# Second products of a four-layer trunk: unit order in layers 2 and 3, order of sum loads, DRAM sums of layer 1, low parts at the seams

## The chip, the cores and the metric

One core of one Trainium2 chip runs the whole program. The metric is the device time of one execution in microseconds (us), from its start to its end. The profiler's span, from the first to the last instruction, is a little shorter than that time. The core has TensorE (PE: matmuls, with weight loads shown apart as PEld), VectorE (DVE), ScalarE (ACT), GpSimd (POOL) and SyncE (SP). SP does nothing here but issue DMAs; ACT and POOL issue a few. A letter q behind an engine's name (SPq, DVEq) means its instruction queue.

## The reference

Four layers act on x of 256 rows and 1024 columns in float32. A layer adds a mixer's output to x (retention, convolution, stick-breaking, retention again) and then that of a feed-forward product:

```python
def squared_relu_mlp(xn, w1, w2):
    h = jax.nn.relu(xn @ w1)
    return (h * h) @ w2
...
        x = x + m
        x = x + squared_relu_mlp(rms_norm(x, norm_ffn[i]), ffn_w1[i], ffn_w2[i])
    return rms_norm(x, final_norm)
```

w1 is 1024 x 4096, w2 4096 x 1024. The change touches the second product, (h * h) @ w2, of each layer, and the places where its end meets the next layer (the seams).

## The kernel before

**Weights.** Every weight is read from DRAM in tiles called raw, 128 x 2048 float32 (1 MB), in an order fixed ahead of time (the plan); a chunk is one such tile, and chunks are numbered through the program. A float32 product is made of three passes: a weight or an activation is cut into a rounded high part and what is left, the low part, and high x high, high x low and low x high are summed (`triple` in `down`). For a weight tile ACT writes the high part (a CAST into wh) and DVE the low part (a subtraction into wl). Pools hold three raw tiles, five wh, five wl and ten 128 x 512 tiles named t. A tile is loaded again once its last reader is done, so a late reader on DVE or ACT delays an SP load, and all loads behind it on SP's queue.

**Second product.** `down` (L770 on) adds up four accumulators C[t, c] (t: half of the rows, c: half of the columns). w2 has 16 blocks kb of 256 rows, and the table MIXED gives the order in which most are used. A *plain* block takes two weight tiles, made by `unit`, and 24 matmuls of 128 x 512. A *fast* block is done as one step of Strassen's scheme (`fast_unit`, L425 on): seven products P1 to P7 of three matmuls each, on seven 128 x 512 operands. Of these, two lie in the first half of the raw tile (low part: L399), two in its second half (L436), and three are sums of blocks of w2, named t3, t2 and t4 (L435 makes the high part, L436 the low part). P5 takes t3, P6 t2, P7 t4; t4 is always t2 plus a block of raw and is made on DVE (L463). P1, P4, P5 and P6 go to four accumulators of their own (mis). Behind the last entry of MIXED, kb 15, ACT copies P1 and P4 out of them (e1 and e5, L827 and L828), and DVE combines all into C (L829 to L834). The remaining plain blocks, REST, follow for c = 0 and then for c = 1.

**Sums made ahead in DRAM.** For a fast block, up to three of its sums of weights are made in DRAM by `make_sums` (L402 on): ACT issues a DMA that writes one block into a DRAM buffer, m or two times over, and POOL issues a DMA that adds other blocks onto it. AHEAD lists, for each layer, at which chunk each of these jobs is issued, and m: 1 gives only the second-half operand t1, 2 also t3, 3 also t2. `unit_hi` then loads raw in two parts, 768 KB from w2 and 256 KB from the buffer, and t3 and t2 as 256 KB loads (t<-sums). With m of 1 or 0, `sum_ahead` (L415 on) makes t3 in SBUF: SP loads one block into a t tile (L421), and POOL adds the second by DMA (L422); each `fast_unit` starts the next one's.

**Order.** Each engine works through its instructions in order. A scheduler arranges them from the program; `issue_after(x)` puts an instruction behind x.

**Seams.** `middle` (L855 on) passes hooks to `down`, which scale finished accumulators (L875 on ACT, L877 on DVE, L906 on DVE), transpose them on PE (`turn`, L888) and add them to x (`onto`, L895), while the plain blocks of REST still run. The next layer's first weight tiles are made at the same time.

Of the kernel before, what the change touches and what calls it, by code (L numbers as in the profile page):

```python
# [56 lines left out]


FAST = 2 * [(3, 5, 7, 9, 12, 13, 14, 15)] + 2 * [(3, 5, 7, 9, 11, 12, 13, 14, 15)]
MIXED = 2 * [(0, 1, 3, 5, 2, 7, 9, 4, 12, 13, 6, 14, 15)] + 2 * [(0, 1, 3, 5, 2, 7, 9, 11, 4, 12, 13, 14, 15)]  # L60
REST = 2 * [(8, 10, 11)] + 2 * [(6, 8, 10)]
AHEAD = {
    0: [(n, 2) for n in (26, 27, 28, 38, 40, 42, 45)],
    1: [(n, 1) for n in (81, 83, 85, 87, 89, 91)],
    2: [(n, 3) for n in (112, 114, 116, 118, 120, 128, 131, 134, 137)],
    3: [(n, 3) for n in (167, 170, 173, 176, 179, 182, 192, 196, 199)],
}
# [186 lines left out]
class Trunk:  # L254
    def __init__(self, ctx, tc, xT, w, prm, cst, fin, gn, out):
        self.tc, self.nc = tc, tc.nc
        self.w_d, self.out_d, self.x_d, self.fin_d, self.gn_d = w, out, xT, fin, gn
        pool = lambda name, bufs, **k: ctx.enter_context(tc.tile_pool(name=name, bufs=bufs, **k))
        self.cp = pool("cp", 1)
        self.raw = pool("raw", 3)  # L260
        self.wp = pool("wp", 5)
        self.zp = pool("zp", 1)
        self.big = pool("big", 36)
        self.t2 = pool("t2", 10)
        self.colp = pool("colp", 3)
        self.bc = pool("bc", 2)
        self.prp = pool("prp", 3)
        self.dram = pool("dram", 2, space=bass.MemoryType.DRAM)
        self.acc_p = pool("acc", 4, space=bass.MemoryType.PSUM)
        self.mis_p = pool("mis", 4, space=bass.MemoryType.PSUM)  # L270
        self.n = 0
        self.un = 0
        self.rest = self.end = None
        self.sums, self.later, self.made = [], [], {}
        nc = self.nc
        head = self.cp.tile([P, NP0 + 512], F32, name="head", tag="head")
        self.prm0 = head[:, :NP0]
        self.x = [head[:, NP0:]]
        self.prm = self.cp.tile([P, NPCOL - NP0], F32, name="prm", tag="prm")
        self.cst = self.cp.tile([P, CCOL["D"]], F32, name="cst", tag="cst")  # L280
        self.first = [self.raw.tile([P, RAWW], F32, name=f"raw{n}", tag="raw") for n in range(3)]
        self.ones = self.tmp().bitcast(mybir.dt.bfloat16)[:, :512]
        nc.gpsimd.memset(self.ones, 1.0)
        self.warm(11)

        def weights(n, a, b, queue=nc.sync):
            queue.dma_start(self.first[n][:, a:b], w[n][:, a:b])

        weights(0, 0, 512, nc.scalar)
        nc.sync.dma_start(head[:, : NP0 + S], xT[:, : NP0 + S])  # L290
        nc.sync.dma_start(self.x[0][:, S:], xT[:, NP0 + S : NP0 + 512])
        weights(0, 512, 1024)
        for p in range(1, 4):
            self.x.append(self.cp.tile([P, 512], F32, name=f"x{p}", tag=f"x{p}"))
            nc.sync.dma_start(self.x[p], xT[:, NP0 + p * 512 : NP0 + (p + 1) * 512])
            weights(p // 2, p % 2 * 1024, (p % 2 + 1) * 1024)
        for o in range(UPC):
            weights(2, o * 1024, (o + 1) * 1024)
        n = CCOL["D"]
        nc.sync.dma_start(self.cst[:, :n], cst[:, :n])  # L300
        nc.sync.dma_start(self.prm, prm[:, NP0:])
        self.cst_d = cst
        self.cr = {k: self.cp.tile([P, P], F32R, name=f"{k}r", tag=f"{k}r") for k in ("U", "m1", "id", "neg")}
        self.id = self.c("id", P)
# [42 lines left out]
    def unit_hi(self, key):  # L347
        nc = self.nc
        assert PLAN[self.un] == key, (PLAN[self.un], key)
        o = self.un % UPC  # L350
        if o == 0:
            n = self.un // UPC
            if n < len(self.first):
                self.rawt = self.first[n]
            else:
                self.rawt = self.raw.tile([P, RAWW], F32, name=self.nm("raw"), tag="raw")
                h = 1024 if n < 4 else UPC * 1024
                made = self.made.get((key[1], key[3])) if key[2] == "f" else None
                if made:
                    h = 1536  # L360
                parts = [
                    (self.rawt[:, a : a + h], self.w_d[n][:, a : a + h]) for a in range(0, UPC * 1024 // h * h, h)
                ]
                if made:
                    d, m = made
                    parts.append((self.rawt[:, h : h + 512], d[:, :512]))
                    self.fetched = [self.tmp() for _ in range(m - 1)]
                    parts += [(t, d[:, 512 * (a + 1) : 512 * (a + 2)]) for a, t in enumerate(self.fetched)]
                for o, d in parts:
                    load = nc.sync.dma_start(o, d)  # L370
                    if made and key[3] not in FAST[key[1]][:2]:
                        self.tc.keep_in_program_order(load)
            for _ in range(min(2, len(self.later))):
                self.later.pop(0)()
            if self.un // UPC in JOBS:
                self.make_sums(*JOBS[self.un // UPC])
            if self.un // UPC in DECAY:
                i = DECAY.index(self.un // UPC) % RH
                if i == 0:
                    self.decay = self.cp.tile([P, RH * 384], F32, name=self.nm("decay"), tag="decay")  # L380
                n = i * 384
                self.tc.keep_in_program_order(
                    nc.sync.dma_start(self.decay[:, n : n + 384], self.cst_d[:, CCOL["D"] + n : CCOL["D"] + n + 384])
                )
        o = self.un % UPC
        src = self.rawt[:, o * 1024 : (o + 1) * 1024]
        hi = self.wp.tile([P, 1024], F32R, name=self.nm("wh"), tag="wh")
        lo = self.wp.tile([P, 1024], F32R, name=self.nm("wl"), tag="wl")
        n = 512 if self.un < 2 * UPC else 1024
        cuts = [slice(i, i + n) for i in range(0, 1024, n)]  # L390
        for s in cuts:
            nc.scalar.copy(hi[:, s], src[:, s])  # L392
        self.un += 1
        return hi, lo, src, cuts

    def unit_lo(self, u):
        hi, lo, src, cuts = u
        for s in cuts:
            self.lo_ins = self.nc.vector.tensor_sub(lo[:, s], src[:, s], hi[:, s]).ins  # L399
        return hi, lo  # L400


# [23 lines left out]
    def fast_unit(self, name, l, kb):  # L426
# [32 lines left out]
                t2 = self.tmp()  # L459
                nc.vector.tensor_add(t2, t1, b22)  # L460
        t4 = self.tmp()
        parts(t3, t2)
        nc.vector.tensor_add(t4, t2, b21)  # L463
        parts(t4)
        return [out[i] for i in (1, 0, 2, 3, 4, 5, 6)]


# [311 lines left out]
    def down(self, i, h, fast, begin, hook):  # L779
# [15 lines left out]
        C = {}  # L795
# [42 lines left out]
        if i == 0:  # L838
# [7 lines left out]

            self.later = [fetch] * len(self.strips)

        for c in range(2):
            w, late = {}, late_kb[-2] if c else late_kb[-1] + 1  # L850
            steps = [(kb, kk, t) for kb in late_kb if kb < late for kk in range(2) for t in range(2)]
            steps += [(kb, kk, t) for t in range(2) for kb in late_kb if kb >= late for kk in range(2)]
            for kb, kk, t in steps:
                if kb not in w:
                    with self.tc.issue_after(closed) if c else nullcontext():  # L855
                        w[kb] = plain(kb, c)
                if c:
                    hook(C, (kb, kk, t))
                triple(C[t, c], block(2 * kb + kk, t), w[kb][kk], stop=(kb, kk) == (late_kb[-1], 1))
            if c == 0:  # L860
                with self.tc.issue_after(closed):
                    hook(C, 0)
        return C


    def middle(self, i, h, fast, sums, nxt):
# [24 lines left out]
        def onto(p, *t):  # L891
            x, a = (v3(b, 2, S) for b in (self.x[p], pt[p]))
            if t:
                x, a = (b[:, :, t[0] * P : (t[0] + 1) * P] for b in (x, a))
            nc.vector.tensor_add(x, x, a)  # L895

        def hook(C, at):
            if at == "open":
# [4 lines left out]
            if at == 0:  # L903
                for t, op in enumerate((ALU.add, ALU.subtract)):
                    y[t, 0] = self.tmp()
                    nc.vector.scalar_tensor_tensor(  # L906
                        out=y[t, 0], in0=C[t, 0], scalar=r2[:, t : t + 1], in1=y["open", t], op0=ALU.mult, op1=op
                    )
                self.norm_begin()
            if at == (REST[i][1], 0, 0):  # L910
                for t in range(2):
                    turn(t, 0)
                for p in range(2):
                    onto(p)
                    self.norm_pair(p, *nxt, False)
                    self.norm_sq(p, nc.vector)
            if at == (REST[i][-2], 0, 1):
# [4 lines left out]
                    onto(p, 0)  # L922

        C = self.down(i, h, fast, None, hook)
        scaled(C, 1, 1, (slice(0, S), "act"), (slice(S, 512), "dve"))

        def rest():
# [943 lines left out]
```

## Time and profile before

| what | value |
|---|---|
| median of three runs | 1336.99 us (1332.95 to 1337.97) |
| the profiled execution | 1336.21 us |
| its span, first to last instruction | 1334.4 us |
| mean granted TensorE clock | 0.996 |
| busy: PE, DVE, ACT, POOL | 98%, 82%, 66%, 16% |
| DMA queue of SP | 259.74 MB |
| DMA queue of POOL | 31.20 MB |
| DMA queue of ACT | 17.30 MB |

The profile is one execution. Its page has the busy time of each engine, the span cut into slices, and the chain of work that ended last: from the last instruction back, at each step to what released it or to the instruction before it on its engine. Further views of the trace are the waits (who waited for whom, in total, how often, the longest), stretches (busy time of each engine between two times, and the clock granted to TensorE), and the timeline (instructions in order of time, runs of alike ones merged, with the idle time ahead of them and its releaser in brackets). "mis" and "acc" are accumulators, "in_w" the weights in DRAM, "sums" the DRAM buffers, "big" 128 x 512 tiles. A matmul of 128 x 512 is listed with 0.39 us because it overlaps its neighbours; PE starts one every 0.227 us.

### The profile page before, as it was taken

How to read it: one execution, taken by the hardware profiler on the slowest of the kernel's cores; microseconds unless marked ns; L12 is line 12 of the kernel's file. 1: busy time of each engine (PE TensorE's matmuls, PEld its weight loads, DVE VectorE, ACT ScalarE, POOL GpSimd, SP SyncE). 2: the span in 40 equal slices, each digit the busy share in tenths (PEclk: the TensorE clock that was granted, in tenths of full speed). 3: DMA queues.
4: the chain of work that ended last, by engine and by line, in shares of the span. 5: the costliest groups of instructions: out<-in, count | busy, mean ns of one | idle time of the engine just before them, and what ended most of it. 6: DMA issues, size and time to landing. Idle time of an engine off the chain costs nothing.

```text
span 1334.4 us, 20667 instructions
## 1 busy us (share of the span) xinstructions
PE 1311.9 (98%) x7661; PEld 1126.7 (84%) x7661; DVE 1089.1 (82%) x1903; ACT 883.1 (66%) x1451; POOL 213.4 (16%) x240
## 2 busy tenths in 40 slices
PE   9999999999999999989999999999999999999998
PEld 7988888888899898868788898887888888888886
DVE  7988777888888588769888588878898667799977
ACT  7555556886666478856668678866766554667764
POOL 3554421000019010010001110100031101101000
PEclk9999999999999999989999999999999999999999
DMA  8566786887675657788578858997566888569883
GB/s 308 212 209 234 250 254 207 238 259 256 235 296 138 210 173 232 216 218 268 188 218 218 237 171 260 270 287 263 203 222 216 256 252 262 192 215 275 260 290 111
DMA packets 76037, 309.57 MB, mean 232 GB/s; under 512 B 8480, under 2 KB 13728, under 8 KB 52512
## 3 DMA queue, kind: packets, MB, share of 16 engines
q1 hardware_dynamic: 55888, 259.74, 54.9%
q0 software_dynamic: 11520, 31.20, 12.0%
q10 hardware_dynamic: 8528, 17.30, 5.3%
q8 instruction: 60, 0.98, 0.3%
q14 instruction: 41, 0.34, 0.1%
HBM read 301.57 MB, written 45.45 MB: 260 GB/s over the span
## 4 chain that ended last, share of the span: by engine, by line
PE 88%; DMA 6%; DVE 3%; ACT 1%; issue 1%; SPq 1%; DVEq 0%; POOLq 0%; ACTq 0%
PE acc L647 22%; PE acc L643 11%; PE acc L784 11%; PE acc L1220 6%; PE acc L1222 6%; PE acc L1221 6%; PE mis L784 5%; DMA t<-sums 3%; PE acc L627 3%; PE acc L628 3%; PE acc L629 3%; PE mis L647 2%; DVE wl L399 1%; DMA t<-in_w 1%; PE acc L1388 1%; PE mis L643 1%
## 5 line engine op out<-in xcount | busy, mean ns | idle before, releaser
L399 DVE TENSOR_TENSOR wl<-raw,wh 128x1024 fp32r<-128x1024 f32 (+1 forms) x406 | 495.9, 1235 | 97.9 <-ACT wh L392 96.3
L392 ACT CAST wh<-raw 128x1024 fp32r<-128x1024 f32 (+1 forms) x406 | 418.8, 1041 | 193.7 <-PE acc L1222 63.4
L647 PE MATMUL acc<-z,wh 128*128 128x512 f32 x1152 | 399.1, 393 | 0.0
L643 PE MATMUL acc<-z,wl 128*128 128x256 f32 x1152 | 317.7, 280 | 0.0
L647 PEld LDWEIGHTS acc<-z,wh 128*128 128x128 f32 x1152 | 214.2, 187 | 46.8
L643 PEld LDWEIGHTS acc<-z,wl 128*128 128x128 f32 x1152 | 216.9, 189 | 2.4 <-DVE t L672 0.3
L784 PE MATMUL acc<-wh,big 128*128 128x512 f32 x632 | 208.8, 391 | 0.0
L784 PEld LDWEIGHTS acc<-wh,big 128*128 128x128 f32 x632 | 118.8, 188 | 24.5
L1220 PE MATMUL acc<-wh,z 128*128 128x512 f32 x352 | 138.4, 394 | 0.0
L1222 PE MATMUL acc<-wh,z 128*128 128x512 f32 x352 | 137.3, 390 | 0.0
L1221 PE MATMUL acc<-wl,z 128*128 128x512 f32 x352 | 137.2, 390 | 0.0
L784 PE MATMUL acc<-wl,big 128*128 128x512 f32 x316 | 123.3, 390 | 1.6 <-DVE wl L436 1.6
L435 ACT CAST wh<-t 128x512 fp32r<-128x512 f32 x102 | 60.4, 619 | 51.9 <-DMA t<-in_w 12.1
L410 POOL DMA_DIRECT2D sums<-in_w x31 | 27.2, 888 | 373.1 <-DMA sums<-in_w 373.1
L671 ACT COPY t<-acc 128x256 f32<-128x256 f32 x154 | 53.1, 371 | 49.3 <-PE acc L647 47.5
L436 DVE TENSOR_TENSOR wl<-t,wh 128x512 fp32r<-128x512 f32 x102 | 65.9, 687 | 17.0 <-ACT wh L435 16.9
L1220 PEld LDWEIGHTS acc<-wh,z 128*128 128x128 f32 x352 | 66.1, 188 | 15.2 <-issue 2.2
L1222 PEld LDWEIGHTS acc<-wh,z 128*128 128x128 f32 x352 | 66.1, 188 | 14.7 <-issue 0.8
L1221 PEld LDWEIGHTS acc<-wl,z 128*128 128x128 f32 x352 | 66.1, 188 | 13.4
L784 PEld LDWEIGHTS acc<-wl,big 128*128 128x128 f32 x316 | 59.5, 188 | 14.6 <-DVE wl L436 2.4
L784 PE MATMUL mis<-wh,big 128*128 128x512 f32 x168 | 64.1, 396 | 5.9 <-ACT wh L435 5.9
L672 DVE TENSOR_TENSOR t<-acc,t 128x256 f32<-128x256 f32 x154 | 59.5, 419 | 10.4 <-ACT t L671 10.0
(309 smaller groups left out, 2358.8 us busy)
## 6 DMA issues: line engine op xcount, KB each, us to landing
raw<-in_w SPq DMA_DIRECT2D x183, 1024.0 KB, 5.3
raw<-in_w SPq DMA_DIRECT2D x31, 768.0 KB, 5.6
sums<-in_w ACTq DMA_DIRECT2D x25, 512.0 KB, 7.5
sums<-in_w POOLq DMA_DIRECT2D x25, 512.0 KB, 9.1
t<-sums SPq DMA_DIRECT2D x43, 256.0 KB, 6.7
raw<-sums SPq DMA_DIRECT2D x31, 256.0 KB, 5.8
sums<-in_w POOLq DMA_DIRECT2D x24, 256.0 KB, 6.6
strip<-st POOLq DMA_DIRECT2D x36, 128.0 KB, 4.0
```

The lines of the kernel that those rows point to most:

```text
L392: nc.scalar.copy(hi[:, s], src[:, s])
L399: self.lo_ins = self.nc.vector.tensor_sub(lo[:, s], src[:, s], hi[:, s]).ins
L435: nc.scalar.copy(h[:, c], t)
L436: self.lo_ins = nc.vector.tensor_sub(g[:, c], t, h[:, c]).ins
L643: mm = nc.tensor.matmul(ps[m][:, :S], wl[:, kk, cs], a[:, :S], start=first and kk == 0, stop=False, **kw)
L647: nc.tensor.matmul(ps[m], wh[:, kk, cs], a, start=False, stop=last and kk == 3, **kw)
L671: nc.scalar.copy(o[:, s], ps[m][:, S:])
L672: nc.vector.tensor_add(o[:, s], ps[m][:, :S], o[:, s])
L784: mm = nc.tensor.matmul(o, l, r, start=start and n == 0, stop=stop and n == 2, skip_group_check=True)
L1220: nc.tensor.matmul(ps[t], zh[:, s], wh[:, kk], start=k == 0, stop=False, skip_group_check=True)
L1221: nc.tensor.matmul(ps[t], zh[:, s], wl[:, kk], start=False, stop=False, skip_group_check=True)
L1222: nc.tensor.matmul(ps[t], zl[:, s], wh[:, kk], start=False, stop=k == 7, skip_group_check=True)
```

## The change

Five edits.

1. MIXED of layers 2 and 3 is reordered: kb 3 and 5 follow kb 0 directly, and fast blocks stand in groups of at most three.
2. AHEAD of layer 1 had six jobs of m = 1 at chunks 81 to 91; it has seven of m = 2 at chunks 77 to 89. `sum_ahead` is left with one block of layer 1, kb 15.
3. Where t3 and t2 come from DRAM, they are loaded ahead of their raw tile.
4. In `fast_unit` t4 moves back among DVE's instructions: with m = 3 behind the low part of raw's second half, otherwise behind t2's low part. The parts of a block are chained by `issue_after`.
5. At a seam the low parts of the next layer's first tiles are held behind the addition to x of the first two pairs of columns (`hold`), and the last tile of REST for c = 1 is made behind the scaling of C for c = 0 (`first`).

```diff
-MIXED = 2 * [(0, 1, 3, 5, 2, 7, 9, 4, 12, 13, 6, 14, 15)] + 2 * [(0, 1, 3, 5, 2, 7, 9, 11, 4, 12, 13, 14, 15)]
+MIXED = 2 * [(0, 1, 3, 5, 2, 7, 9, 4, 12, 13, 6, 14, 15)] + 2 * [(0, 3, 5, 1, 7, 9, 2, 11, 12, 4, 13, 14, 15)]
...
-    1: [(n, 1) for n in (81, 83, 85, 87, 89, 91)],
+    1: [(n, 2) for n in (77, 79, 81, 83, 85, 87, 89)],
...
-                    parts += [(t, d[:, 512 * (a + 1) : 512 * (a + 2)]) for a, t in enumerate(self.fetched)]
+                    extra = [(t, d[:, 512 * (a + 1) : 512 * (a + 2)]) for a, t in enumerate(self.fetched)]
+                    parts = extra + parts
...
         for s in cuts:
-            self.lo_ins = self.nc.vector.tensor_sub(lo[:, s], src[:, s], hi[:, s]).ins
+            with self.tc.issue_after(self.hold) if self.hold else nullcontext():
+                self.lo_ins = self.nc.vector.tensor_sub(lo[:, s], src[:, s], hi[:, s]).ins
...
         t4 = self.tmp()
-        parts(t3, t2)
-        nc.vector.tensor_add(t4, t2, b21)
-        parts(t4)
+        if m == 3:
+            with self.tc.issue_after(self.lo_ins):
+                self.lo_ins = nc.vector.tensor_add(t4, t2, b21).ins
+        with self.tc.issue_after(self.lo_ins):
+            parts(t3, t2)
+        if m < 3:
+            with self.tc.issue_after(self.lo_ins):
+                nc.vector.tensor_add(t4, t2, b21)
+        with self.tc.issue_after(self.lo_ins):
+            parts(t4)
...
+        first = None
         for c in range(2):
...
                 if kb not in w:
-                    with self.tc.issue_after(closed) if c else nullcontext():
+                    after = first if first and kb == late_kb[-1] else closed if c else None
+                    with self.tc.issue_after(after) if after else nullcontext():
                         w[kb] = plain(kb, c)
...
             if c == 0:
                 with self.tc.issue_after(closed):
-                    hook(C, 0)
+                    first = hook(C, 0)
...
                 for p in range(2):
-                    onto(p)
+                    y["on"] = onto(p)
...
         C = self.down(i, h, fast, None, hook)
+        self.hold = y["on"]
```

The order of three engines shows where instructions stand now. The first place is SP in layer 1, from the load of kb 5's raw tile to that of kb 7's. In the kernel before (the t<-in_w loads at L421 are for POOL's additions):

```order
L370 DMA raw_6749<-in_w 128x1536
L370 DMA raw_6749<-sums_6017 128x512
L370 DMA raw_6798<-in_w 128x2048
L421 DMA t_1330_6618<-in_w 128x512
L421 DMA t_1331_6621<-in_w 128x512
L421 DMA t_1349_6703<-in_w 128x512
L421 DMA t_1365_6756<-in_w 128x512
L370 DMA raw_6832<-in_w 128x1536
L370 DMA raw_6832<-sums_6146 128x512
```

and in the changed one, where line numbers are one or two higher:

```order
L371 DMA raw_6748<-in_w 128x1536
L371 DMA raw_6748<-sums_5763 128x512
L371 DMA raw_6796<-in_w 128x2048
L423 DMA t_1331_6621<-in_w 128x512
L371 DMA t_1347_6697<-sums_5642 128x512
L371 DMA t_1363_6749<-sums_5763 128x512
L371 DMA t_1380_6831<-sums_5893 128x512
L371 DMA raw_6830<-in_w 128x1536
L371 DMA raw_6830<-sums_5893 128x512
```

Three of the four 256 KB loads now read finished sums of DRAM; POOL's DMA behind each of them is gone. The number of loads up to this point is the same.

The second place is DVE in layer 2, two fast blocks that follow each other (kb 7 and 9 in both). Before, t4 of the second (L463) stands ahead of low parts of the first:

```order
L399 TENSOR_TENSOR wl_9910<-raw_9902,wh_9909 128x1024
L463 TENSOR_TENSOR t_2091_9965<-t_2086_9952,raw_9950 128x512
L436 TENSOR_TENSOR wl_9914<-raw_9902,wh_9913 128x1024
L436 TENSOR_TENSOR wl_9919<-t_2073_9903,wh_9918 128x512
L436 TENSOR_TENSOR wl_9919<-t_2074_9904,wh_9918 128x512
L436 TENSOR_TENSOR wl_9926<-t_2079_9917,wh_9925 128x512
L463 TENSOR_TENSOR t_2103_10013<-t_2098_10000,raw_9998 128x512
L399 TENSOR_TENSOR wl_9958<-raw_9950,wh_9957 128x1024
```

Now each block's t4 (L466) stands within the block:

```order
L401 TENSOR_TENSOR wl_9872<-raw_9864,wh_9871 128x1024
L438 TENSOR_TENSOR wl_9876<-raw_9864,wh_9875 128x1024
L466 TENSOR_TENSOR t_2075_9879<-t_2070_9866,raw_9864 128x512
L438 TENSOR_TENSOR wl_9882<-t_2069_9865,wh_9881 128x512
L438 TENSOR_TENSOR wl_9882<-t_2070_9866,wh_9881 128x512
L438 TENSOR_TENSOR wl_9888<-t_2075_9879,wh_9887 128x512
L401 TENSOR_TENSOR wl_9920<-raw_9912,wh_9919 128x1024
```

What DVE waits for at t4 is its own block's t2, which SP loads ahead of that block's raw tile now, and behind it before.

The third place is ACT at the end of layer 0's second product: the last fast block, kb 15 (raw_3864), then the first tiles of REST (raw_3928). Before:

```order
L435 CAST wh_3871<-raw_3864 128x1024
L435 CAST wh_3878<-t_712_3347 128x512
L435 CAST wh_3878<-t_835_3875 128x512
L435 CAST wh_3885<-t_836_3877 128x512
L392 CAST wh_3934<-raw_3928 128x1024
L827 COPY big_3910<-mis_3449 128x512
L392 CAST wh_3950<-raw_3928 128x1024
L828 COPY big_3911<-mis_3450 128x512
```

and now:

```order
L437 CAST wh_3871<-raw_3864 128x1024
L437 CAST wh_3878<-t_712_3347 128x512
L437 CAST wh_3878<-t_835_3875 128x512
L836 COPY big_3910<-mis_3449 128x512
L837 COPY big_3911<-mis_3450 128x512
L437 CAST wh_3885<-t_836_3877 128x512
L393 CAST wh_3934<-raw_3928 128x1024
L393 CAST wh_3950<-raw_3928 128x1024
```

The copies of P1 and P4 (mis_3449 and mis_3450) have moved ahead of the high part of t4 (t_836) and of the first tile of REST. Layer 1 has the same order; in layers 2 and 3 only the copy of P1 stands ahead of t4's high part.

At the seam from layer 1 to layer 2, DVE did the two scalings of L906, three low parts (L399) and then the two additions to x; now the two scalings, one low part and the additions, and three low parts behind them.

More of the change, by code (lines that the diff above doesn't have):

```diff
@@ L272, in __init__ @@
         self.un = 0
-        self.rest = self.end = None
+        self.rest = self.end = self.hold = None
         self.sums, self.later, self.made = [], [], {}
@@ L894, in onto @@
                 x, a = (b[:, :, t[0] * P : (t[0] + 1) * P] for b in (x, a))
-            nc.vector.tensor_add(x, x, a)
+            return nc.vector.tensor_add(x, x, a).ins
         def hook(C, at):
@@ L905, in hook @@
                     y[t, 0] = self.tmp()
-                    nc.vector.scalar_tensor_tensor(
+                    last = nc.vector.scalar_tensor_tensor(
                         out=y[t, 0], in0=C[t, 0], scalar=r2[:, t : t + 1], in1=y["open", t], op0=ALU.mult, op1=op
@@ L909, in hook @@
                 self.norm_begin()
+                return last.ins
             if at == (REST[i][1], 0, 0):
```

## The prediction

> **What bounds the kernel now.** I read the page first: busy time, then the chain that ended last.
>
> ```profile
> PE 1311.9 (98%) x7661; PEld 1126.7 (84%) x7661; DVE 1089.1 (82%) x1903; ACT 883.1 (66%) x1451; POOL 213.4 (16%) x240
> ...
> PE 88%; DMA 6%; DVE 3%; ACT 1%; issue 1%; SPq 1%; DVEq 0%; POOLq 0%; ACTq 0%
> ```
>
> PE is busy for all but 22.5 us of the span of 1334.4, and the change keeps every matmul. So only PE's idle time, and what a slow restart adds to it, can be won. The view of PE's waits says where that is (what PE waited for: us in total, times, longest):
>
> ```profile
> PE mis L784 <- ACT wh L435: 5.9, 1, 5.9
> PE mis L1406 <- issue: 2.8, 2, 2.1
> PE mis L888 <- ACT t L875: 2.4, 2, 1.4
> PE acc L784 <- DVE wl L436: 1.6, 2, 1.0
> PE mis L784 <- DVE wl L399: 1.5, 3, 1.2
> ```
>
> L784 is the second product, L888 the seams' transposes; L1406 isn't touched. The four rows in reach hold 11.4 us. The largest is one stop of 5.9 us, and the chain of waits shows its cause (start, us, what):
>
> ```profile
> 570.23 0.14 SPq L370
> ...
> 570.42 10.33 DMA t<-in_w
> ...
> 581.33 7.99 DMA t<-in_w
> ```
>
> This is layer 1's first t3: SP's load waited for free t tiles until 570.23, then POOL's addition took 8 us more, one after the other. PE's timeline around it:
>
> ```profile
> 583.76 0.39 PE L784 MATMUL mis<-wh,big 128*128 128x512 f32 x1
> 590.01 0.79 PE L784 MATMUL mis<-wh,big 128*128 128x512 f32 x1 [5.86 <-ACT wh L435]
> ...
> 593.71 0.39 PE L784 MATMUL acc<-wh,big 128*128 128x512 f32 x1
> ```
>
> **The change part by part.** All is summed against the profiled execution, 1336.21 us, which is 0.78 under the median of 1336.99.
>
> *Layer 1's sums.* The undisturbed pace is in layer 0's last fast block:
>
> ```profile
> 357.08 0.39 PE L784 MATMUL mis<-wh,big 128*128 128x512 f32 x1
> ...
> 358.67 0.39 PE L784 MATMUL acc<-wh,big 128*128 128x512 f32 x1
> 358.90 0.39 PE L784 MATMUL acc<-wl,big 128*128 128x512 f32 x1
> ```
>
> From 357.08 to 358.67 are seven matmuls, 0.227 us each. From 583.76 to 593.71 PE started nine, worth 2.04 us, in 9.95: the stop with its slow restart costs **7.9 us**. The granted clock fell with it (stretch; length, then busy time and instructions of PE, PEld, DVE, ACT and POOL; granted clock; DMA share; GB/s):
>
> ```profile
> 294.08:358.83 64.75, 64.75 (x286) 53.61 (x287) 55.98 (x80) 41.86 (x59) 1.95 (x4) 1.00 0.71 235
> 580.00:600.00 20.00, 14.14 (x55) 10.95 (x54) 9.84 (x12) 9.03 (x12) 4.43 (x5) 0.83 0.82 201
> 900.00:920.00 20.00, 18.81 (x83) 15.06 (x82) 16.58 (x20) 12.54 (x16) 0.00 (x0) 1.00 0.80 282
> ```
>
> [...]
>
> With m = 2 kb 3's t3 comes in one load, and neither POOL's 7.99 us nor its wait remains. Layer 0 has the same MIXED and m = 2 already: in the first of these stretches PE is busy for all 64.75 us. So I take the whole 7.9. Are the sums there in time? ACT issues the jobs about 11.3 us apart, and the page has their two halves:
>
> ```profile
> 510.96 0.55 ACTq L409 DMA_DIRECT2D sums<-in_w  x1
> ...
> sums<-in_w ACTq DMA_DIRECT2D x25, 512.0 KB, 7.5
> sums<-in_w POOLq DMA_DIRECT2D x25, 512.0 KB, 9.1
> ```
>
> The first job moves from chunk 81 to 77, two jobs or some 22 us ahead of 510.96, and needs 16.6 us: done near 505, and first read behind 570. The doubled traffic lies beside PE's work; SP's later loads have slack, below.
>
> *Order in layers 2 and 3.* There the stops are on DVE's low parts, behind t4:
>
> ```profile
> DVE t L463 <- DMA t<-sums: 21.3, 16, 3.0
> ...
> 900.47 0.69 DVE L463 TENSOR_TENSOR t<-t,raw 128x512 f32<-128x512 f32 x1 [1.25 <-DMA t<-sums]
> ...
> 902.36 0.50 PE L784 MATMUL mis<-wl,big 128*128 128x512 f32 x1 [1.19 <-DVE wl L399]
> ```
>
> t4 of a *later* block waits for its t2, and the low part that PE needs now stands behind it. The five stops of this kind are the rows with L399 and L436: 1.5 + 1.6 = 3.1 us. With t2 loaded ahead of its raw tile, about one block (4.8 us) earlier, and t4 back in its own block, a wait of at most 3.0 us goes: **-3.1**. Bounds: 0, if the DVE waits merely move, and 3.1.
>
> The new order also puts kb 3 straight behind kb 0, which asks for t3 and t2 5.4 us (24 matmuls) sooner than before. Layer 2's start:
>
> ```profile
> 863.62 0.33 SPq L370 DMA_DIRECT2D raw<-in_w  x1
> ...
> 867.58 0.56 DVE L747 TENSOR_TENSOR sum<-t,sum 128x384 fp32r<-128x384 f32 x1
> ...
> 869.77 0.48 PE L784 MATMUL acc<-wh,big 128*128 128x512 f32 x1
> ...
> 870.58 2.38 SPq L370 DMA_DIRECT2D t<-sums  x4
> ...
> 879.37 0.69 DVE L463 TENSOR_TENSOR t<-t,raw 128x512 f32<-128x512 f32 x1 [0.15 <-DMA t<-sums]
> ```
>
> Before, these loads stood behind a raw tile that waited for kb 1's low part. Now that tile waits for kb 0's, done by 863.62, and the loads for a t tile that DVE gives back about when it starts L747 at 867.58. So they go about 3 us sooner, and t2, read at 879.37 before, is there near 876.3. DVE then adds t4 (0.69) and makes t3's low part (0.69) by 877.7; P5's second matmul, 37 matmuls behind kb 0's first at 869.77, wants it at 878.2. A margin of 0.5 beside DVE's other work there is thin. Bounds: 0, and 2.5 if the loads are not sooner (879.37 + 1.3 against 878.2). I take **+0.3**, nearest to the dependencies.
>
> *ACT at the end of layers 0 and 1.* The copy of P4 (e5) now stands ahead of t4's high part, so ACT waits for P4 of the same block. In layer 0:
>
> ```profile
> 357.99 0.58 ACT L828 COPY big<-mis 128x512 f32<-128x512 f32 x1
> 358.46 3.20 ACT L392 CAST wh<-raw 128x1024 fp32r<-128x1024 f32 x3
> ...
> 936.15 0.39 PE L784 MATMUL mis<-wh,big 128*128 128x512 f32 x1
> ...
> 936.58 0.59 ACT L828 COPY big<-mis 128x512 f32<-128x512 f32 x1 [0.24 <-PE mis L784]
> ```
>
> The last two rows, from layer 2, show that the copy can start 0.43 behind the start of P4's last matmul: in layer 0 at 357.08 + 0.43 = 357.51. The copy takes 0.58, the 512-wide CAST 0.62 (t4's high part at 358.6), DVE's low part 0.69: ready at 359.34, wanted at 358.90. Stop 0.45. REST's first CAST is then done at 359.6, and its low part, behind a subtraction of e1 on DVE (0.69 + 1.22), at 361.07; wanted at 360.03. Stop 1.0. Together 1.45 in each of layers 0 and 1: **+2.9**. Bounds: 0, if PE's operands have more cover than this walk gives them, and 3.8 if both steps slip by another 0.45. In layers 2 and 3 only e1's copy stands there, whose P1 is long done: nothing.
>
> *Seams.* At the seam from layer 1 to 2:
>
> ```profile
> 655.83 1.23 DVE L399 TENSOR_TENSOR wl<-raw,wh 128x1024 fp32r<-128x1024 f32 x1 [0.20 <-ACT wh L392]
> 656.98 0.68 DVE L895 TENSOR_TENSOR head<-head,mis 128x512 f32<-128x512 f32 x1
> ...
> 661.07 0.66 PE L888 MATMUL mis<-cst,t 128*128 128x128 f32 x4 [1.44 <-ACT t L875]
> ```
>
> The additions to x waited for two low parts; with them moved behind, the additions come near 655.6, 1.4 sooner, and so does ACT's scaling: nearly all of the 1.44 goes. But three low parts (3 x 1.23) now stand ahead of DVE's remaining seam work, on which the last transposes wait. An estimate puts 0.75 of these 3.7 us on the path, since PE has REST's matmuls to do meanwhile. Net **-0.6**; bounds -1.4 and +2.3 (3.7 less 1.4). The other two seams stay: there the additions came straight behind the scaling already.
>
> Sum: -7.9 - 3.1 + 0.3 + 2.9 - 0.6 = -8.4. 1336.21 - 8.4 = 1327.8; beside the median, **1328.5**.
>
> **The rivals.**
>
> A. *ACT's copies cost nothing*: 1328.5 - 2.9 = 1325.6. For it: a walk by hand of 0.4 us margins. Against it: the copy's wait is in the order itself.
>
> B. *The gains in layers 2 and 3 are given back at their starts and at the seam*: 2 x 2.5 - 0.3 for the starts and 0.6 for the seam, 1333.8. For it: the margin of 0.5.
>
> C. *The change of AHEAD doesn't do what it says*: the t<-sums loads still wait for t tiles, or sums come late, and the stop stays: 1328.5 + 7.9 = 1336.4. Against it: the load alone is 8 us shorter than load and addition.
>
> D. *Raw tiles come late in layers 2 and 3*, since two 256 KB loads stand ahead of each: 512 KB at 282 GB/s is 1.8 us, and their issue 1.2. From
>
> ```profile
> 913.13 0.33 SPq L370 DMA_DIRECT2D raw<-in_w  x1
> ...
> 922.33 1.05 ACT L392 CAST wh<-raw 128x1024 fp32r<-128x1024 f32 x1
> ```
>
> a tile has 9.2 us from issue to first use, and lands in some 5.7: slack 3.5 for 3.0. If it fails by 1 us for a third of the 18 blocks, 1334.5. [...]
>
> E. *Slower*: DVE becomes the bound in layers 0 and 1. t4 is added behind t2's low part there, so DVE waits for ACT's CAST of t4 in every fast block: 0.62 + 0.03 on top of some 5.7 (two adds of 0.69, two low parts of 1.22, three of 0.63), 6.35 against PE's 21 x 0.227 = 4.77. A block whose lead is spent costs 1.6; all 16 would make 1354, and from 10 on it is slower by over 0.5%. Against it: with 8 x 0.65 more DVE has 61.2 of layer 0's 64.75 us, and plain blocks give lead back.
>
> **How the numbers follow.** Forecast 0.46, A 0.17, B 0.14, C 0.07, D 0.06, E 0.10. A measurement of this kernel tells about 0.5% from no change: 1330.3 and 1343.7. Faster are A and most of the forecast (0.40): 0.57. The forecast's rest, B, C and D are within: 0.33. Slower: 0.10. The range leaves out E and the fringe of A: low 1323 (A with the seam's full gain), high 1337 (C and the runs' own spread).
>
> **What would show it.** The stop near 590 and the clock of 0.83 gone, layer 1's stretch near 64.8 us; L463's successors no longer ahead of a stop in layers 2 and 3; two new stops at the end of layers 0 and 1, on t4's low part and on REST's first, with ACT waiting for P4 at the copy; the seam's 1.44 shrunk. Wrong would be: stops inside fast blocks of layers 0 and 1 (E), ACT waiting for raw (D), or a stop at kb 3 in layer 2 or 3 (B).

## The result, and the profile after

| | before | changed |
|---|---|---|
| median | 1336.87 us (5 runs, 1332.95 to 1337.97) | 1327.43 us (5 runs, 1326.19 to 1329.32) |
| profiled execution | 1336.21 us | 1327.43 us |
| its span | 1334.4 us | 1325.5 us |

The ratio is 0.9937, with a 95% interval from 0.9918 to 0.9955: 9.4 us less, where 8.4 were forecast. In the page of the changed kernel PE is busy for all but 15.2 us, and DMA has shrunk from 6% to 1% of the chain that ended last:

```profile
span 1325.5 us, 20664 instructions
PE 1310.3 (99%) x7661; PEld 1124.6 (85%) x7661; DVE 1091.6 (82%) x1902; ACT 878.7 (66%) x1451; POOL 201.1 (15%) x234
...
PE 95%; DVE 2%; DMA 1%; ACT 1%; issue 0%; SPq 0%; ACTq 0%; DVEq 0%
```

PE's waits of the changed kernel (what it waited for: us in total, times, longest) no longer have the 5.9 us for ACT. The second product (now L793) still waits for DVE's low parts, but in layers 0 and 1, where it did not before, and no longer in layers 2 and 3:

```profile
PE acc L793 <- DVE wl L401: 2.0, 3, 0.8
...
PE mis L899 <- ACT t L886: 0.8, 1, 0.8
PE acc L793 <- DVE wl L438: 0.5, 2, 0.2
...
PE mis L899 <- DVE t L888: 0.2, 1, 0.2
```

To see where each layer gained, I took for each the stretch from the start of its first to the start of its last matmul of the second product, from the timeline. It holds the seam's scalings and most of its transposes. The rows give the stretch, its length, busy time of each engine, granted clock, DMA share and GB/s. Before, layers 0 to 3:

```profile
293.94:377.99 84.05, 83.09 (x374) 68.64 (x374) 74.02 (x105) 53.35 (x74) 2.07 (x5) 1.00 0.77 268
570.25:662.72 92.47, 85.17 (x374) 69.57 (x373) 75.06 (x105) 53.17 (x74) 8.61 (x10) 0.96 0.77 236
869.77:955.91 86.14, 83.79 (x370) 67.58 (x370) 71.07 (x100) 55.49 (x76) 2.16 (x3) 1.00 0.82 273
1244.50:1327.55 83.05, 82.32 (x368) 67.60 (x366) 67.70 (x100) 52.19 (x73) 0.81 (x1) 1.00 0.64 220
```

and in the changed kernel:

```profile
293.93:381.07 87.14, 84.87 (x373) 68.09 (x373) 73.92 (x103) 52.27 (x74) 2.08 (x5) 1.00 0.73 256
572.83:658.29 85.46, 84.47 (x373) 68.16 (x373) 72.87 (x100) 52.45 (x74) 1.71 (x2) 1.00 0.65 223
865.89:948.10 82.21, 82.21 (x370) 68.04 (x370) 70.70 (x99) 54.20 (x76) 2.97 (x4) 1.00 0.79 274
1236.98:1318.68 81.70, 81.70 (x367) 67.74 (x366) 68.45 (x100) 51.06 (x73) 0.81 (x1) 1.00 0.63 220
```

Layer 1 gains 7.0 us, layer 2 3.9 and layer 3 1.35; layers 2 and 3 have no idle PE left. Layer 0 *loses* 3.1, though its second product had no stop before. The 192 to 289 us between these stretches change by 0.6 or less each.

The loss is best seen at the end of layer 0's second product, where the prediction expected two stops. Timelines of the changed kernel (start, us, what, idle time before and its releaser): first DVE, then ACT, then PE.

```profile
357.49 1.29 DVE L438 TENSOR_TENSOR wl<-t,wh 128x512 fp32r<-128x512 f32 x2
358.70 0.68 DVE L471 TENSOR_TENSOR t<-t,raw 128x512 f32<-128x512 f32 x1
360.23 0.69 DVE L438 TENSOR_TENSOR wl<-t,wh 128x512 fp32r<-128x512 f32 x1 [0.85 <-ACT wh L437]
...
361.44 1.22 DVE L401 TENSOR_TENSOR wl<-raw,wh 128x1024 fp32r<-128x1024 f32 x1
```

```profile
359.09 0.59 ACT L837 COPY big<-mis 128x512 f32<-128x512 f32 x1 [1.26 <-PE mis L793]
359.57 0.62 ACT L437 CAST wh<-t 128x512 fp32r<-128x512 f32 x1
```

```profile
360.98 0.50 PE L793 MATMUL acc<-wl,big 128*128 128x512 f32 x1 [0.23 <-DVE wl L438]
...
362.71 0.50 PE L793 MATMUL acc<-wl,big 128*128 128x512 f32 x1 [0.77 <-DVE wl L401]
```

Both stops are there, on t4's low part and on REST's first, and ACT waits for P4 at its copy. But t4's addition (L471) also ends only at 359.38, 0.2 us before the CAST starts: with the copy or without, the CAST had little to gain. In the kernel before, t4 was ready at 354.44, 3.5 us ahead of the copy of P4. Either could be the cause; the experiments take them apart.

### The profile page after: what moved, and what is told of

The parts are those of the page before. It is cut to its first block, busy times and chain, and to the rows that moved or that the text cites. A ratio compares the mean times of both kernels' runs of the same rounds, so it can differ in the third digit from the quotient of the medians.

```text
span 1325.5 us, 20664 instructions
## 1 busy us (share of the span) xinstructions
PE 1310.3 (99%) x7661; PEld 1124.6 (85%) x7661; DVE 1091.6 (82%) x1902; ACT 878.7 (66%) x1451; POOL 201.1 (15%) x234
## 4 chain that ended last, share of the span: by engine, by line
PE 95%; DVE 2%; DMA 1%; ACT 1%; issue 0%; SPq 0%; ACTq 0%; DVEq 0%
PE acc L656 22%; PE acc L793 17%; PE acc L652 11%; PE mis L793 7%; PE acc L1233 6%; PE acc L1235 6%; PE acc L1234 6%; PE acc L636 3%; PE acc L637 3%; PE acc L638 3%; PE mis L656 2%; PE acc L1401 1%; PE mis L652 1%; PE acc L1534 1%; DMA big<-in_gn 1%; DVE wl L401 1%
## 5 line engine op out<-in xcount | busy, mean ns | idle before, releaser
L793 PE MATMUL acc<-wh,big 128*128 128x512 f32 x632 | 209.0, 392 | 0.0
L793 PEld LDWEIGHTS acc<-wh,big 128*128 128x128 f32 x632 | 118.7, 188 | 24.7 <-ACT wh L437 0.5
L793 PE MATMUL acc<-wl,big 128*128 128x512 f32 x316 | 124.1, 393 | 2.5 <-DVE wl L401 2.0
L793 PEld LDWEIGHTS acc<-wl,big 128*128 128x128 f32 x316 | 59.4, 188 | 18.0 <-DVE wl L401 5.2
L636 PE MATMUL acc<-z,wh 128*128 128x256 f32 x224 | 63.7, 284 | 0.0
```

The source lines that it names most:

```text
L636: nc.tensor.matmul(o, wh[:, kk, cs], ah, start=st, stop=False, **kw)
L793: mm = nc.tensor.matmul(o, l, r, start=start and n == 0, stop=stop and n == 2, skip_group_check=True)
```

## The experiments

Twelve runs followed, eleven of other kernels and one of the changed kernel again. This table has each one's stretches as above (us, layers 0 to 3) and its time; single times vary by some us for causes elsewhere (the part between layer 0's and layer 1's stretch alone took 190.7 to 194.8 us), so the stretches carry the verdicts.

| kernel | 0 | 1 | 2 | 3 | time (us) |
|---|---|---|---|---|---|
| before | 84.05 | 92.47 | 86.14 | 83.05 | 1336.87 |
| changed | 87.14 | 85.46 | 82.21 | 81.70 | 1327.43 |
| changed again | 87.14 | 84.79 | 82.21 | 81.70 | 1325.95 (4 runs) |
| t4 early | 83.84 | 82.91 | 82.22 | 81.70 | 1319.29 (4 runs) |
| copy behind | 87.85 | 88.66 | 82.21 | 81.70 | 1329.85 (1) |
| copies first, t4 early | 85.54 | 84.60 | 82.22 | 81.69 | 1326.40 (1) |
| sums undone | 85.71 | 94.94 | 82.22 | 81.69 | 1336.03 (1) |
| sums alone | 84.05 | 84.47 | 83.17 | 82.26 | 1325.80 (1) |
| order undone | 87.37 | 85.15 | 82.28 | 81.70 | 1327.50 (1) |
| loads undone | 85.74 | 85.11 | 82.22 | 81.70 | 1327.99 (1) |
| t4's place undone | 83.86 | 82.91 | 82.87 | 81.70 | 1321.19 (1) |
| hold undone | 85.73 | 86.37 | 82.91 | 81.70 | 1326.97 (1) |
| seam undone | 87.71 | 86.71 | 82.86 | 81.69 | 1332.30 (1) |
| two edits | 84.06 | 84.48 | 82.22 | 81.70 | 1321.98 (4 runs) |

**t4 early**: t4's addition back at its old place in layers 0 and 1.

```diff
         if m < 3:
-            with self.tc.issue_after(self.lo_ins):
-                nc.vector.tensor_add(t4, t2, b21)
+            nc.vector.tensor_add(t4, t2, b21)
```

> The changed kernel with t4's addition put back to its old place in layers 0 and 1 only (m below 3). The second product's stretches, first to last matmul, are 87.1, 85.5, 82.2 and 81.7 us in the changed kernel's layers 0 to 3. Theory: the late t4 makes DVE wait for ACT's CAST of it in each fast block, and lets ACT's copies of P1 and P4 slip ahead of that CAST; both go. Layer 0's stretch falls to 84.0 to 84.5, layer 1's to 83.0 to 83.5, no stop on a low part is left there, and the whole falls by 4.5 to 5.5, to about 1322.4. Rival 1 (the chaining of all low parts of a block, not t4's place, costs it): the stops inside the blocks stay and only the copies' go, about 3.3 less, 1324. Rival 2 (t4 early puts off another low part): below 1 us, 1327.

Measured: 1319.29 us, ratio to the kernel before 0.986 (0.9834 to 0.9886), clear of the changed kernel's interval. Layer 0 falls by 3.3 us and layer 1 by 2.55, no low part stops PE, and the time falls by 8.1, more than the 4.5 to 5.5 expected. In the stretches the theory holds. The rest of the 8.1 isn't in the second products: the spans of the two profiled executions differ by 6.1. DVE's timeline of this kernel has t4 (L470) ready before the CAST needs it, and the three low parts without a gap:

```profile
353.96 0.69 DVE L470 TENSOR_TENSOR t<-t,raw 128x512 f32<-128x512 f32 x1
354.57 1.22 DVE L438 TENSOR_TENSOR wl<-raw,wh 128x1024 fp32r<-128x1024 f32 x1
355.71 1.89 DVE L438 TENSOR_TENSOR wl<-t,wh 128x512 fp32r<-128x512 f32 x3
```

**Copy behind**: t4 late as in the changed kernel, P4's copy held behind the CAST of t4.

```diff
-                nc.scalar.copy(h[:, c], t)
+                self.hi_ins = nc.scalar.copy(h[:, c], t).ins
...
-        nc.scalar.copy(e5, p5)
+        with self.tc.issue_after(self.hi_ins):
+            nc.scalar.copy(e5, p5)
```

> The changed kernel with ACT's copy of P4 (e5) held behind the CAST of t4's high part; t4's addition stays late, and the copy still stands ahead of REST's first CAST. Theory of the prediction: the copy is what makes the two stops of 0.23 and 0.77 us at the end of layers 0 and 1; the first goes and the second shrinks by half at least, layer 0's stretch falls from 87.1 by 0.6 to 1.0. Rival: t4's addition on DVE ends only 0.3 us before the copy lets the CAST start, so the lateness of t4 is the cause, and the copy merely stands in its shadow: at most 0.3 less per layer, both stops there.

Measured: nothing gained. PE's timeline:

```profile
359.04 0.50 PE L793 MATMUL acc<-wl,big 128*128 128x512 f32 x1 [0.22 <-DVE wl L438]
...
362.10 0.50 PE L793 MATMUL acc<-wl,big 128*128 128x512 f32 x1 [1.86 <-DVE wl L401]
```

The first stop is the same, and ACT's CAST waits for t4's addition there, so the late t4 alone makes it. The second is longer, but this isn't a clean comparison: the scheduler also put three of DVE's combinations of products ahead of REST's first low part, where the changed kernel has one. So for the second stop the late t4 is not shown to be enough, and what the copy does by itself this kernel can't say.

**Copies first**: t4 early, and ACT's order forced to what it is in the changed kernel. The part of `fast_unit` that makes t4's high and low part is called only behind P4 and the copies.

```diff
...
+                if q == 3 and part is not None:
+                    e1, e5 = self.bigt(), self.bigt()
+                    nc.scalar.copy(e1, p1)
+                    w.append(part[0](nc.scalar.copy(e5, p5).ins))
...
```

> The kernel of the run t4_early (stretches of layers 0 and 1: 83.8 and 82.9 us, no stop on a low part), with ACT's two copies forced ahead of the CAST of t4's high part in layers 0 and 1, as they stand in the changed kernel. Theory of the prediction (the copy of P4 alone makes the stops): a stop of about 0.45 us on t4's low part and one of about 1.0 on REST's first, each layer's stretch longer by 1.2 to 1.7. Rival (the lateness of t4's addition alone): no stop over 0.2, both stretches within 0.3 of t4_early's. Between: 0.4 to 1.0 per layer.

Measured, in layer 0:

```profile
359.47 0.50 PE L799 MATMUL acc<-wl,big 128*128 128x512 f32 x1 [0.23 <-DVE wl L438]
...
361.20 0.50 PE L799 MATMUL acc<-wl,big 128*128 128x512 f32 x1 [0.77 <-DVE wl L401]
```

Both stops come back, within 0.01 us, and both layers are 1.7 us longer than with t4 early (83.84 to 85.54, 82.91 to 84.60). So the copies alone are enough for both stops, and the late t4 alone for the first. There the two causes stand in each other's shadow: moving the copy away gains nothing, and t4's old place removes both, since the scheduler then also leaves the copies behind.

**Sums undone and sums alone**: AHEAD of layer 1 as before in the changed kernel, and as in the changed kernel in the one before.

```diff
-    1: [(n, 2) for n in (77, 79, 81, 83, 85, 87, 89)],
+    1: [(n, 1) for n in (81, 83, 85, 87, 89, 91)],
```

> The changed kernel with layer 1's DRAM sums as before (six jobs of m = 1 at chunks 81 to 91). Theory: the stop of 5.9 us at kb 3 of layer 1 and the slow matmuls behind it come back, and layer 1's stretch rises from 85.5 by 7.5 to 8.3, the whole to about 1335.3; layers 2 and 3 don't move by over 0.3. Rival: part of layer 1's gain came from other edits (the chained parts, the seam), and the stretch rises by less than 6.

> The kernel before with layer 1's DRAM sums of the changed one and nothing else. Theory: the 5.86 us stop and its slow matmuls go, 7.9 us in all, and nothing else moves: layer 1's stretch 84.3 to 84.9, layers 2 and 3 at 86.1 and 83.1, the whole near 1328.5. Rival: the larger DRAM traffic takes some of it back, a stop at another block of layer 1, or later loads; layer 1's stretch above 85.5.

Measured: undone, a stop of 5.81 us is back at kb 3 and another of 0.77 at kb 15, and layer 1's stretch rises by 9.5, more than expected. Most of the excess is the clock: in the 7 us behind the stop of 5.8 us PE had 18 matmuls at a granted clock of 0.59, where the kernel before (second row) had 23 at 0.75. Five matmuls of 0.227 us are 1.1 us; the stop of 0.77 comes on top.

```profile
590.28:597.28 7.00, 7.00 (x18) 5.27 (x19) 6.06 (x9) 4.17 (x7) 0.86 (x1) 0.59 0.48 85
590.01:597.01 7.00, 7.00 (x23) 5.36 (x24) 6.83 (x10) 5.37 (x8) 0.86 (x1) 0.75 0.58 109
```

Alone, layer 1's stretch falls from 92.47 to 84.47, **8.0 us**, where 7.9 were worked out, with no new stop. The rival of contention is out. But layers 2 and 3 moved too, by 3.0 and 0.8, though nothing was changed there. In that kernel DVE still waits for t2 at t4, and PE's timeline has two short stops left:

```profile
DVE t L463 <- DMA t<-sums: 16.6, 12, 3.1
...
915.18 0.50 PE L784 MATMUL mis<-wl,big 128*128 128x512 f32 x1 [0.32 <-DVE wl L399]
...
1286.93 0.50 PE L784 MATMUL mis<-wl,big 128*128 128x512 f32 x1 [0.23 <-DVE wl L399]
```

Every engine has the same order of instructions in these two layers as in the kernel before. So the stops there depend on when the loads land in an execution (16.6 us of waits for t2 here, 21.3 in the kernel before): in the profiled one of the kernel before they cost 5.3 us, here 1.5 (83.17 + 82.26 against 82.21 + 81.70). These are one execution each.

**Order undone, loads undone, t4's place undone**: one of the three edits that meet in layers 2 and 3 taken back in the changed kernel, in this order: MIXED, the loads ahead of raw, and t4's place in all layers.

```diff
-... + 2 * [(0, 3, 5, 1, 7, 9, 2, 11, 12, 4, 13, 14, 15)]
+... + 2 * [(0, 1, 3, 5, 2, 7, 9, 11, 4, 12, 13, 14, 15)]
```

```diff
-                    parts = extra + parts
+                    parts += extra
```

```diff
-        if m == 3:
-            with self.tc.issue_after(self.lo_ins):
-                self.lo_ins = nc.vector.tensor_add(t4, t2, b21).ins
-        with self.tc.issue_after(self.lo_ins):
-            parts(t3, t2)
-        if m < 3:
-            with self.tc.issue_after(self.lo_ins):
-                nc.vector.tensor_add(t4, t2, b21)
-        with self.tc.issue_after(self.lo_ins):
-            parts(t4)
+        parts(t3, t2)
+        nc.vector.tensor_add(t4, t2, b21)
+        parts(t4)
```

> The changed kernel with the old order of blocks in layers 2 and 3 alone. Theory: sums loaded ahead of raw and t4 in its own block are enough; no stop over 0.3 us comes back in layers 2 and 3, whose stretches stay at 82.2 and 81.7 within 0.4. Rival: four fast blocks in a row (12 to 15) use up DVE's lead, 5.0 us a block against PE's 4.77, and one or two stops on low parts come back in the last of them, 0.5 to 1.5 us in each layer.

> The changed kernel with t3 and t2 loaded behind their raw tile again, t4 still within its own block. Theory 1 (t4's place is enough, since a block later t2 has landed): no stop over 0.2 us in layers 2 and 3, stretches 82.2 and 81.7 within 0.4. Theory 2 (the early loads are needed): DVE waits for t2 at t4 again, over 5 us in total in layers 2 and 3, and stops of 0.5 us or more come back, 1 to 3 us per layer.

> The changed kernel with the whole of edit 4 undone (t4 where the scheduler puts it, ahead of the low parts of the block before, in all layers; parts not chained), loads still early. Layers 2 and 3: by theory 1 (t4's place matters) stops come back, 1 to 3 us per layer; by theory 2 (the early loads are enough) none over 0.2, 82.2 and 81.7 within 0.4. Layers 0 and 1: 83.8 and 82.9 as in t4_early within 0.3, if t4's place and not the chain was what cost there.

Measured: the order does nothing by itself, 82.28 and 81.70. Without the early loads nothing comes back either (82.22 and 81.70): t4 in its own block is enough, and DVE waits for t2 once, 1.8 us. With the early loads and t4 at its old place one stop of 0.31 us remains in layer 2, near its start:

```profile
870.68 0.50 PE L786 MATMUL mis<-wl,big 128*128 128x512 f32 x1 [0.31 <-DVE wl L401]
```

So either edit takes nearly all of the stops, and t4's place all of them. In the last kernel layers 0 and 1 are at 83.86 and 82.91, as with t4 early: t4's place and not the chaining of the parts costs there.

**Hold undone and seam undone**: the changed kernel without the hold, and without the whole of edit 5.

```diff
-        self.hold = y["on"]
```

```diff
-                    after = first if first and kb == late_kb[-1] else closed if c else None
+                    after = closed if c else None
```

The second kernel has both of these diffs.

> The changed kernel without the hold at the seams: two low parts of layer 2's first tiles stand ahead of the additions to x again. The seam from layer 1 to 2 has one stop of 0.23 us in the changed kernel where the kernel before had one of 1.44. Theory: the hold is what took it; a stop of 1.0 to 1.5 us comes back there, and layer 1's stretch with its seam grows by 0.6 to 1.3. Rival (the later first tile of REST, or the faster layer 1, took it): stop below 0.5, no difference over 0.3.

> The changed kernel with the whole of edit 5 undone: no hold, and REST's last tile for c = 1 not behind the scaling. Theory: at the seam from layer 1 to 2 the full stop of 1.4 comes back (0.50 without the hold alone, 0.23 with both), layer 1's stretch grows from 85.5 to 86.5 to 87.0. Rival: REST's last tile does nothing; 0.5 as without the hold.

Measured at the seam from layer 1 to 2, without the hold and without both:

```profile
656.82 0.66 PE L899 MATMUL mis<-cst,t 128*128 128x128 f32 x4 [0.50 <-ACT t L886]
```

```profile
661.54 0.66 PE L899 MATMUL mis<-cst,t 128*128 128x128 f32 x4 [1.70 <-ACT t L886]
```

In the changed kernel this stop for ACT is gone, and one of 0.23 us for DVE stands 2 us behind the end of the stretch. So more of the gain at this seam is the later tile of REST (1.70 to 0.50) than the hold (0.50 to 0.23). The stretch rises by 0.9 without the hold, but the part behind it, to layer 2's first matmul, falls by 0.5 (207.60 to 207.08), so the hold is worth some 0.4 us here, less than the 0.7 by which this stretch differs between two executions of the changed kernel (85.46 and 84.79). That the hold took the stop of 1.44 has fallen. But it also acts at the seam from layer 2 to 3. Without it layer 2's stretch is 0.7 longer (82.91), with a stop there that the changed kernel doesn't have:

```profile
946.80 0.66 PE L899 MATMUL mis<-cst,t 128*128 128x128 f32 x4 [0.51 <-ACT t L886]
```

**Two edits**: the kernel before with the new AHEAD of layer 1 (its diff as above), and with t4 within its own block where m = 3; nothing else.

```diff
...
-        parts(t3, t2)
-        nc.vector.tensor_add(t4, t2, b21)
-        parts(t4)
+        if m == 3:
+            with self.tc.issue_after(self.lo_ins):
+                self.lo_ins = nc.vector.tensor_add(t4, t2, b21).ins
+            with self.tc.issue_after(self.lo_ins):
+                parts(t3, t2)
+            with self.tc.issue_after(self.lo_ins):
+                parts(t4)
+        else:
+            parts(t3, t2)
+            nc.vector.tensor_add(t4, t2, b21)
+            parts(t4)
```

> The kernel before with two edits only: layer 1's DRAM sums as in the changed kernel, and t4 within its own block in layers 2 and 3 (m = 3) alone. No new order of blocks, no early loads, no seam edit, t4 of layers 0 and 1 at its old place. Theory: these two carry the change's gain. Stretches of the second product 84.0, 84.6 (92.5 less 7.9), 82.2 and 81.7 us; the sum falls against before by 7.9 + 3.9 + 1.35, to about 1323. Rival: the early loads or the order are needed beside them; layers 2 or 3 keep over 0.5 us of stops and the whole stays above 1325.

Measured: 1321.98 us, ratio 0.9906 (0.9882 to 0.9929), stretches as expected. Two of the five edits carry more than the whole gain. By the medians t4 early is another 2.7 better, with intervals (0.9834 to 0.9886 against 0.9882 to 0.9929) that just touch; the seam's edit is what it has besides that moved a stop.

**Changed again**: the changed kernel once more.

> The changed kernel itself, for its own spread: stretches 87.1 (or 85.7, as in three kernels whose layer 0 is the same, if its stop of 0.50 at the first plain block behind two fast ones comes and goes), 85.3, 82.2 and 81.7 us; time near 1327.4.

Measured: 1325.95 us, ratio 0.9931 (0.9909 to 0.9953). Layer 0 is at 87.14 again. Three kernels with t4 late and the copies ahead were at 85.7 there, without a stop of 0.5 us that this and three others show at the first plain block behind kb 3 and 5. The engines' order in layer 0 is the same in the changed kernel and in sums undone, of which one has the stop and the other hasn't. What differs is when the layer's first t<-sums load lands, as ACT's timelines show, first of the changed kernel, then of sums undone:

```profile
305.17 1.14 ACT L437 CAST wh<-t 128x512 fp32r<-128x512 f32 x2 [4.85 <-DMA t<-sums]
```

```profile
302.26 1.14 ACT L437 CAST wh<-t 128x512 fp32r<-128x512 f32 x2 [2.00 <-DMA t<-sums]
```

The four runs with t4 late and this stop waited 4.85 to 5.21 us there, the four without it (copy behind is the fourth) 1.80 to 3.02. With t4 early the wait was 4.75 and no stop followed. So it takes both: the load that lands late and the late t4.

## Why the prediction was right

The sum was near (8.4 forecast, 8.9 in the spans), in part by luck: the stops in layers 2 and 3 gave 2.2 more than forecast, and t4's late addition, with the copies, took 3.0 more (5.9 against 2.9). (By its own terms the forecast beside the median is 1328.6; 1328.5 stands there.)

- *Layer 1's sums*, -7.9: right in mechanism and size. Alone they give 8.0, and rival C is out.
- *Stops in layers 2 and 3*, -3.1: right in mechanism, too small against this execution, -5.3. The term took the idle time of the waits alone; that a stop costs no more was my estimate. The first matmuls behind these stops are slow too, and the same profile had that: beside the row at 902.36 the next started at 902.70, 0.11 late, and starts of 0.34 instead of 0.23 us also stood ahead of stops. Summed over starts, the stretches before had lost 3.6 and 1.3. It was also one execution's number; another lost 1.5 with the same code.
- *Layer 2's start*, +0.3: nothing; PE never stops in layers 2 and 3. Rival B, losses at these starts and at the seam, is out.
- *ACT's copies*, +1.45 each in layers 0 and 1: the stops came at the two places named, 0.23 and 0.77 us where 0.45 and 1.0 were worked out; with the slow starts behind them 1.7 a layer. The mechanism is shown by the kernel with the copies first, and with it rival A is out. But the step took it for the only one: t4's addition, moved behind t2's low part, was costed nowhere but in rival E, and at the first stop it makes the CAST just as late.
- *Rival E* was thus partly real: DVE does wait for the CAST of t4 in every fast block of layers 0 and 1, 0.76 to 0.85 us in all but the first of each. But DVE doesn't become the bound: beside the two stops at the end of a layer, PE lost by it 1.4 us in layer 0, on some executions. Taking t4 back gains 5.9 us in the two stretches, 3.4 of them (2 x 1.7) at the stops that the copies alone make too.
- *Seam from layer 1 to 2*, -0.6: one stop of 1.44 became one of 0.23, so about -1.2; the three held low parts cost less than the 0.75 that I put on the path (the part behind the stretch grew by 0.5). The part credited to the hold came mostly from REST's last tile.
- *Rival D*: raw tiles do come later. In ACT's waits of the changed kernel, and then of the one before:

```profile
ACT wh L393 <- DMA raw<-in_w: 15.7, 12, 3.6
```

```profile
ACT wh L392 <- DMA raw<-in_w: 1.8, 4, 0.7
```

  But only two of the 12 waits, 0.31 and 1.69 us, lie in the second products of layers 2 and 3, and PE doesn't stop for them. The largest (3.62, 2.85 and 1.87) stand at the ends of layers 0 and 1, and most of the total stays where the loads stand behind raw again (loads undone):

```profile
ACT wh L393 <- DMA raw<-in_w: 12.4, 8, 3.6
```

  So the early loads are not what makes most of it, and D is out.

## What to carry to other kernels

Where a result goes to another engine and back (DVE adds, ACT rounds, DVE subtracts), issue the addition early and let other work fill the gap; one addition moved behind its neighbours, with two copies that the scheduler then put ahead, cost 5.9 us in two layers here. Two causes of one wait can hide each other: taking away the visible one may gain nothing (the first stop was 0.23 us long, and 0.22 with the copy behind), so test each with the other gone. Price a stop of PE by the starts of its matmuls and not by the idle time alone (in layers 2 and 3 before, 3.1 us of idle time and 4.9 by the starts), and take the cost of stops that hang on a DMA's landing from more than one execution (5.3 and 1.5 us here, with the same order of instructions).

## What the runs showed of the hardware that I had not expected

The granted clock fell behind stops of less than 2 us, in some executions. In the kernel with the copy behind, the stretch of the stop of 1.86 us and the two behind it:

```profile
359.75:362.10 2.35, 0.49 (x2) 0.18 (x1) 2.35 (x4) 2.35 (x3) 0.12 (x1) 1.00 0.97 398
362.10:366.10 4.00, 4.00 (x11) 3.13 (x12) 4.00 (x6) 2.60 (x4) 0.00 (x0) 0.57 1.07 409
366.10:370.10 4.00, 4.00 (x19) 3.31 (x18) 2.29 (x3) 1.89 (x2) 0.00 (x0) 1.00 1.05 410
```

For 4 us the clock was 0.57, with 11 matmuls where the next 4 us have 19; behind a stop of 1.85 in layer 1 PE took 3.75 us for nine matmuls, which at 0.227 us each are worth 2.04. Behind one of 1.70 (seam undone) the clock was 1.00 over the next 3.5 us. Length alone doesn't decide it, as two stops in layer 1's mixer show, with matmuls of other shapes. In the kernel before, the 4 us behind a stop of 2.06 us had a clock of 1.00 (first row). With the copies first, the 8 us behind one of 1.70 had 0.66 and 0.50:

```profile
451.62:455.62 4.00, 4.00 (x35) 3.06 (x35) 0.00 (x0) 0.37 (x1) 0.00 (x0) 1.00 0.74 308
```

```profile
445.72:449.72 4.00, 3.99 (x56) 3.17 (x57) 1.93 (x12) 0.68 (x2) 0.00 (x0) 0.66 0.99 391
449.72:453.72 4.00, 4.00 (x56) 2.97 (x60) 2.31 (x11) 1.56 (x5) 0.00 (x0) 0.50 0.91 327
```

Nor is a short stop shortly ahead needed: no stop of over 0.1 us stood in the 9 us ahead of that one. So the clock fell behind stops of 1.70 and 1.86 us, and not behind others of 1.70 and 2.06; what decides is open.
